# A decoder layer: the mask products leave TensorE, and the lambda steps go behind the last pair

## The chip, the cores and the metric

The kernel runs on one core of a Trainium2 chip. The metric is the device time of one execution in microseconds (us). A core has five engines with queues of their own: TensorE (PE, products, with PEld for its weight loads), VectorE (DVE), ScalarE (ACT), GpSimd (POOL) and SyncE (SP, which here only issues loads).

## The reference

One layer of a hybrid decoder for 512 tokens of width 1024. After a norm, a projection feeds eight stick-breaking heads and four differential heads, whose outputs go through `w_o`; then come a feed-forward part with a causal convolution, a gated embedding part and a last norm. The change concerns the stick-breaking heads, and the order of the lambdas of the differential heads:

```python
def block(args):                       # stick-breaking, one block of queries
    past = key_pos[None, :] < q_pos[:, None]
    z = einsum('bhqd,bhkd->bhqk', q_blk, k) * scale
    log_not = where(past, log_sigmoid(-z), 0.0)
    between = cumsum(log_not, axis=3, reverse=True) - log_not
    w = where(past, exp(log_sigmoid(z) + between), 0.0)
    return einsum('bhqk,bhkd->bhqd', w, v)
...
lam = exp(sum(lambda_q1 * lambda_k1)) - exp(sum(lambda_q2 * lambda_k2)) + lambda_init
w = probs[:, :, 0] - lam * probs[:, :, 1]     # differential heads
```

So the weight of key s for query t is sigmoid(z) times the product of sigmoid(-z) over the keys between s and t, and zero where s is not before t.

## The kernel before

Every 32-bit product is made as three products of split operands, high by high, high by low and low by high (`mm3`, L119 to L123). A weight block is loaded to `wraw`, cast to `whi` on ACT (L140), and the rest `wlo` is subtracted on DVE (L141). The text calls the three products of one 128x512 output and one block of 128 input rows a *unit*; the call `self.units(n)` takes the next n units from a flow of projection pieces: q and k of a pair of heads (`add_qk`, L377, its results scaled by DVE and split by ACT and DVE at L387 to L389), v of all pairs (`add_v`, L408, results split at L506 to L511), and so on, eight units for each q or k. PSUM has four banks of tag `mm` for units and two double banks of tag `z` for logits, transposes and head outputs.

A *pair* is two stick-breaking heads. `pair_steps` (L549) makes the logits of a pair in three groups of query blocks: block 3 (512 keys); blocks 2 and 0 (384 and 128 keys); block 1 (256 keys). `logits` (L482) ends a group with two products (L500), one for each head, of the identity with `maskR`, which add a large negative number at the unseen keys of the diagonal blocks. `sb_sticks` (L514) then works on a group: ACT makes sigmoid(-z) into `cum` (L524) and sigmoid(z) into `beta` (L525), DVE runs `cum` backwards as a running product that starts anew where `fresh` is one (a scan, L531, in pieces of 512), and multiplies `beta` by it (L532). Scans of groups 0 and 1 use the two `cum` buffers. `pair_out` (L561) transposes the result (L576), splits it (`split_t`, L542) and multiplies by v (L588), adds the parts of the two heads (L594, L595) and splits the output (L597, L598).

In `stages` (L713) PE follows the order in which the program is written: two units, the broadcast of the first norm to a row (`bcast_rstd1`, L154 and L158), the late evictions of q and k of pair 0, six units, and then a plan of steps of the four pairs with units between them (L820 to L827; an entry is pair, step, units). Other engines run in an order that a scheduler works out at build time; `issue_after` places work behind given instructions. `params` (L199 to L257) is called at one point of the plan (entry 8). It loads gains, convolution weights, lambdas and a one-hot table by loads that ACT issues (L229, L250), sums the lambda products on DVE (L233), takes exponentials on ACT (L238), and combines them (L241); it also makes the bias strips of the differential heads. These heads come after the pairs (`diff_steps`, L601).

Of the kernel before, what the change touches and what calls it, by code (L numbers as in the profile page):

```python
# [41 lines left out]
class Kern:  # L42
# [121 lines left out]
    def consts(self):  # L164
# [17 lines left out]
        zero = su.tile([P, P], F32, name="zero")  # L182
        nc.gpsimd.memset(zero, 0.0)
        msk = su.tile([P, P], F32, name="msk")

        nc.gpsimd.affine_select(msk, zero, pattern=[[-1, P]], compare_op=ALU.is_gt, fill=NEG, base=0, channel_multiplier=1)
        self.maskR = c.tile([P, P], F32R, name="maskR")
        nc.vector.tensor_copy(self.maskR, msk)
# [10 lines left out]
    def params(self, pst):  # L199
        nc, a, c = self.nc, self.a, self.cpool  # L200
# [12 lines left out]
        nc.scalar.dma_start(rows2[0 : 4 * FT, :], a["conv_w"][0, 1:3].rearrange("t (r p) -> (t r) p", p=P))  # L213
        self.par = c.tile([P, n1], F32, name="par1")
# [9 lines left out]


        rest = next(spare)
        lt = rest[:, : 4 * HD].rearrange("p (a d) -> p a d", a=4)
        for i, key in enumerate(("lambda_q1", "lambda_k1", "lambda_q2", "lambda_k2")):
            nc.scalar.dma_start(lt[:, i, :], a[key].partition_broadcast(P).rearrange("p o d -> p (o d)"))  # L229
        s = c.tile([P, 2], F32, name="lsum")  # L230
        junk = rest[:, 4 * HD : 5 * HD]
        for i in range(2):
            nc.vector.tensor_tensor_reduce(  # L233
                out=junk, in0=lt[:, 2 * i, :], in1=lt[:, 2 * i + 1, :], scale=1.0, scalar=0.0,
                op0=ALU.mult, op1=ALU.add, accum_out=s[:, i : i + 1],
            )
# [5 lines left out]


        tab = c.tile([NBUCK + 1, NMAP], F32, name="tab")
        nc.gpsimd.memset(tab, NEG)
        nc.scalar.dma_start(tab[0:NBUCK, :], a["rel_bias"])
        sk = self.dram.tile([NMAP, YW], F32, name="sk")
        for lo, n in ((0, T), (T, P)):
            oh, y = next(spare)[: NBUCK + 1, :n], next(spare)[:NMAP, :n]
            nc.scalar.dma_start(oh, a["onehot"][:, lo : lo + n])  # L250
# [6 lines left out]
        nc.scalar.dma_start(self.sk2, bass.AP(sk.tensor, sk.offset, [[YW, NMAP], [0, P], [1, YW]]))  # L257
# [78 lines left out]
    def behind_x(self, do):  # L336

        with self.tc.issue_after(self.last[0]), self.tc.issue_after(self.last[1]):
            do()
# [142 lines left out]
    def logits(self, q, k, blocks, mask=False):  # L482
# [4 lines left out]
        for at, (tb, col) in enumerate(blocks):  # L487
            n = (tb + 1) * P
            for i, (x, y) in enumerate(((0, 1), (1, 0), (0, 0))):
                for h in range(2):  # L490
# [3 lines left out]
                        start=i == 0 and at == 0, stop=i == 2 and at == len(blocks) - 1 and not mask, skip_group_check=True,  # L494
                    )
        if mask:

            d = [col // P + tb for tb, col in blocks]
            for h in range(2):
                nc.tensor.matmul(  # L500
                    z[:, h, :].rearrange("p (a b) -> p a b", b=P)[:, d[0] : d[-1] + 1, :], lhsT=self.identR,
                    rhs=self.maskR.unsqueeze(1).to_broadcast([P, len(d), P]), start=False, stop=True, skip_group_check=True,
                )
# [10 lines left out]
    def sb_sticks(self, z, g):  # L514
# [27 lines left out]
    def split_t(self, ps, n, c=""):  # L542
        nc = self.nc
        hi, lo = (x[:, :n] for x in self.parts("tw", c))
        nc.scalar.copy(hi, ps[:, :n])  # L545
        nc.vector.tensor_sub(lo, ps[:, :n], hi.bitcast(F32))  # L546
        return hi, lo

    def pair_steps(self, pair):  # L549
# [3 lines left out]
        zs = [self.logits(q, k, ((3, 0),), True), self.logits(q, k, ((2, 0), (0, 3 * P)), True)]  # L553
# [3 lines left out]
        self.sb_sticks(self.logits(q, k, ((1, 0),), True), 2)  # L557
# [155 lines left out]
    def stages(self):  # L713
# [56 lines left out]
        def begin(i):  # L770
            self.behind_x(lambda: self.prepare(i))
# [16 lines left out]
        self.behind_x(self.norm_x)  # L788
# [19 lines left out]
        self.fresh = self.work.tile([P, 6 * P], F32, name="fresh", bufs=1)  # L808
        nc.gpsimd.memset(self.fresh, 0.0)
        nc.gpsimd.memset(self.fresh[:, 3 * P : 3 * P + 1], 1.0)  # L810
        self.v[0] = self.vp.tile([P, NB, 2 * T], F32R, tag="v", name="v_sb")

        self.units(2)
# [19 lines left out]

# [219 lines left out]
```

## Time and profile before

| | before |
|---|---|
| median of 3 runs, us | 706.27 |
| lowest and highest, us | 704.77, 706.96 |
| profiled execution, us | 706.06 |
| its span, us | 704.3 |
| PE busy, us (share) | 685.5 (97%) |
| DVE busy, us (share) | 441.1 (63%) |
| ACT busy, us (share) | 313.8 (45%) |
| POOL busy, us (share) | 42.5 (6%) |

The span is counted from the first to the last event that the profiler recorded; the execution's own time is 1.8 us longer. In a row of a timeline the first number is the start in us, the second the duration; x6 means that six alike stand in the row together. The bracket gives the time for which the engine had been idle and who released it. A matmul's recorded duration overlaps the next one's start, so distances between starts tell the pace.

### The profile page before, as it was taken

The numbers are of one execution on the slowest core, as the hardware profiler recorded it, in microseconds if no ns is written. First come the engines' busy times: TensorE is split into PE (matmuls) and PEld (weight loads), VectorE is DVE, ScalarE is ACT, GpSimd is POOL, SyncE is SP. The second block draws the span as 40 slices with busy tenths as digits, with TensorE's granted clock in tenths as the row PEclk, the third lists the DMA queues.
The fourth block names the chain that finished last, engine by engine and source line by source line (L and its number), as shares of the span: only waits on it lengthen the run. The fifth ranks groups of instructions, "written<-read, shape, count | busy, mean of one in ns | idle before, by whom it ended". The sixth has DMA issues, their size and how long they took to land. (4 is left out here: it accounts for less than half of the span.)

```text
span 704.3 us, 8244 instructions
## 1 busy us (share of the span) xinstructions
PE 685.5 (97%) x3263; PEld 562.3 (80%) x3263; DVE 441.1 (63%) x663; ACT 313.8 (45%) x471; POOL 42.5 (6%) x52
## 2 busy tenths in 40 slices
PE   8879999999999999999999999999999999999995
PEld 8668877787888887888888888888888888888885
DVE  3775769668666858498777777677734232436445
ACT  4654435556553543365444444444423232326422
POOL 2200000000100024100000000000000020202001
PEclk9989999999999999999999999999999999999999
DMA  9522135232326111223322233321323133127002
GB/s 288 200 69 60 60 108 192 60 94 76 106 85 209 61 60 60 90 90 121 119 77 86 78 120 119 97 84 60 123 101 105 61 104 120 45 92 239 29 27 93
DMA packets 66809, 71.64 MB, mean 102 GB/s; under 512 B 2360, under 2 KB 55850, under 8 KB 66771
## 3 DMA queue, kind: packets, MB, share of 16 engines
q1 hardware_dynamic: 63376, 64.76, 28.8%
q10 hardware_dynamic: 2755, 4.27, 1.8%
q0 software_dynamic: 640, 2.10, 0.8%
q8 instruction: 25, 0.41, 0.3%
q14 instruction: 13, 0.11, 0.0%
HBM read 66.90 MB, written 6.84 MB: 105 GB/s over the span
## 5 line engine op out<-in xcount | busy, mean ns | idle before, releaser
L140 ACT CAST whi<-wraw 128x1024 fp32r<-128x1024 f32 (+1 forms) x102 | 105.5, 1034 | 151.0 <-PE mm L122 128.3
L141 DVE TENSOR_TENSOR wlo<-wraw,whi 128x1024 fp32r<-128x1024 f32 (+1 forms) x102 | 123.5, 1211 | 74.4 <-ACT whi L140 73.4
L121 PE MATMUL mm<-xgh,whi 128*128 128x512 f32 x128 | 53.9, 421 | 0.2 <-DVE v_sb L511 0.2
L122 PE MATMUL mm<-xgl,whi 128*128 128x512 f32 x128 | 51.6, 403 | 0.0
L123 PE MATMUL mm<-xgh,wlo 128*128 128x512 f32 x128 | 51.4, 401 | 0.0
L878 DVE TENSOR_TENSOR vpad<-mm,rb 128x512 f32<-128x512 f32 x44 | 30.1, 688 | 33.8 <-PE mm L123 33.7
L699 POOL TENSOR_TENSOR sqacc<-sqacc,sq 128x512 f32<-128x512 f32 x14 | 23.1, 1653 | 359.6 <-issue 254.9
L880 ACT ACTIVATE y<-vpad,par,par 128x512 f32<-128x512 f32 x44 | 35.5, 814 | 2.7 <-DVE vpad L878 2.5
L882 DVE SCALAR_TENSOR_TENSOR y<-vpad,par,y 128x512 f32<-128x512 f32 x44 | 33.1, 751 | 1.3
L881 DVE SCALAR_TENSOR_TENSOR y<-vpad,par,y 128x512 f32<-128x512 f32 x44 | 32.8, 746 | 0.0
L121 PEld LDWEIGHTS mm<-xgh,whi 128*128 128x128 f32 x128 | 25.2, 197 | 6.8 <-issue 1.1
L884 ACT ACTIVATE y<-y 128x512 f32<-128x512 f32 x22 | 13.9, 631 | 34.9 <-DVE y L882 34.9
L123 PEld LDWEIGHTS mm<-xgh,wlo 128*128 128x128 f32 x128 | 24.9, 194 | 5.6
L122 PEld LDWEIGHTS mm<-xgl,whi 128*128 128x128 f32 x128 | 25.1, 196 | 4.6 <-DVE xgl L331 0.3
L531 DVE TENSOR_TENSOR_SCAN cum<-cum,fresh 128x512 f32<-128x512 f32 x20 | 23.6, 1212 | 4.2 <-ACT cum L524 4.2
L492 PE MATMUL z<-k,q 64*128 64x512 f32 (+3 forms) x192 | 20.6, 340 | 5.2 <-ACT beta L525 3.7
L121 PE MATMUL mm<-whi,xgh 128*128 128x512 f32 x64 | 25.5, 398 | 0.0
L122 PE MATMUL mm<-wlo,xgh 128*128 128x512 f32 x64 | 25.0, 390 | 0.0
L123 PE MATMUL mm<-whi,xgl 128*128 128x512 f32 x64 | 25.0, 390 | 0.0
L492 PEld LDWEIGHTS z<-k,q 64*128 64x128 f32 x192 | 15.5, 189 | 10.9 <-ACT beta L525 4.2
L636 ACT ACTIVATE pr<-pr,nmx 128x512 f32<-128x512 f32 (+3 forms) x32 | 17.6, 552 | 12.2 <-DVE nmx L632 12.0
L546 DVE TENSOR_TENSOR twl<-z,twh 128x1024 fp32r<-128x1024 f32 (+2 forms) x20 | 18.4, 954 | 7.1 <-ACT twh L545 7.0
(538 smaller groups left out, 1759.4 us busy)
## 6 DMA issues: line engine op xcount, KB each, us to landing
wraw<-in_w_up SPq DMA_DIRECT2D x22, 1024.0 KB, 5.0
wraw<-in_w_in SPq DMA_DIRECT2D x16, 512.0 KB, 5.2
wraw<-in_w_down SPq DMA_DIRECT2D x8, 1024.0 KB, 5.0
wraw<-in_w_in SPq DMA_DIRECT2D x4, 1024.0 KB, 6.1
wraw<-in_w_o SPq DMA_DIRECT2D x4, 1024.0 KB
wraw<-in_w_ple_gate SPq DMA_DIRECT2D x4, 1024.0 KB, 8.2
wraw<-in_w_down SPq DMA_DIRECT2D x4, 768.0 KB, 4.3
sk<-sk ACTq DMA_DIRECT2D x1, 2560.0 KB
```

What stands on the lines that cost most here:

```text
L121: nc.tensor.matmul(ps, lhsT=l[0], rhs=r[0], start=start, stop=False, **kw)
L122: nc.tensor.matmul(ps, lhsT=l[0], rhs=r[1], start=False, stop=False, **kw)
L123: nc.tensor.matmul(ps, lhsT=l[1], rhs=r[0], start=False, stop=stop, **kw)
L140: nc.scalar.copy(hi, raw)
L141: nc.vector.tensor_sub(lo, raw, hi.bitcast(F32))
L492: nc.tensor.matmul(z[:, h, col : col + n], lhsT=q[o, x, tb * P : (tb + 1) * P], rhs=k[o, y, :n], start=i == 0 and at == 0, stop=i == 2 and ...
L531: nc.vector.tensor_tensor_scan(back, back, fresh, 1.0, op0=ALU.mult, op1=ALU.max)
L699: nc.gpsimd.tensor_add(sqacc, sqacc, sq)
L878: nc.vector.tensor_mul(u[:, 2 : T + 2], ps, rb2)
L880: nc.scalar.activation(y, u[:, 2 : T + 2], AF.Identity, scale=self.cw(2, ch), bias=self.g("cb", ch))
L881: nc.vector.scalar_tensor_tensor(y, u[:, 1 : T + 1], self.cw(1, ch), y, op0=ALU.mult, op1=ALU.add)
L882: nc.vector.scalar_tensor_tensor(y, u[:, 0:T], self.cw(0, ch), y, op0=ALU.mult, op1=ALU.add)
```

## The change

The products with `maskR` are gone. Instead, GpSimd builds two tables at the start: `keep`, a 128x128 block of ones where the key comes before the query and zeros elsewhere, and `whole`, which takes the place of `fresh` and has ones at the unseen keys of the diagonal blocks, so that the running product (a product followed by a maximum) is one there. The scans now cover a head's piece each, so the third group has two of 256 instead of one of 512. GpSimd multiplies the diagonal blocks of `beta` by `keep`, four-dimensional views of 128x2x128, 128x2x256 and 128x2x128 elements in the three groups, in place, between ACT's second sigmoid and DVE's product.

`params` becomes a generator whose loads are written at entry 4 of the plan and the rest at entry 8; the lambda steps have a function of their own, called after the split of v of the differential heads and placed behind the last split of a pair. PE gets five units instead of two ahead of the broadcast, and eight instead of eleven in the last entry of the plan.

```diff
-        zero = su.tile([P, P], F32, name="zero")
-        nc.gpsimd.memset(zero, 0.0)
-        msk = su.tile([P, P], F32, name="msk")
-
-        nc.gpsimd.affine_select(msk, zero, pattern=[[-1, P]], compare_op=ALU.is_gt, fill=NEG, base=0, channel_multiplier=1)
-        self.maskR = c.tile([P, P], F32R, name="maskR")
-        nc.vector.tensor_copy(self.maskR, msk)
+        self.keep = c.tile([P, P], F32, name="keep")
+        nc.gpsimd.affine_select(
+            self.keep, self.ones, pattern=[[-1, P]], compare_op=ALU.is_gt, fill=0.0, base=0, channel_multiplier=1
+        )
...
+        rest = next(spare)
+        lt = rest[:, : 4 * HD].rearrange("p (a d) -> p a d", a=4)
+        for i, key in enumerate(("lambda_q1", "lambda_k1", "lambda_q2", "lambda_k2")):
+            nc.scalar.dma_start(lt[:, i, :], a[key].partition_broadcast(P).rearrange("p o d -> p (o d)"))
...
+        yield
...
+    def lambdas(self):
+        nc, c = self.nc, self.cpool
+        s = c.tile([P, 2], F32, name="lsum")
+        for i in range(2):
+            nc.vector.tensor_tensor_reduce(
...
+        e = c.tile([P, 2], F32, name="lexp")
+        nc.scalar.activation(e, s, AF.Exp)
...
-        if mask:
-
-            d = [col // P + tb for tb, col in blocks]
-            for h in range(2):
-                nc.tensor.matmul(
-                    z[:, h, :].rearrange("p (a b) -> p a b", b=P)[:, d[0] : d[-1] + 1, :], lhsT=self.identR,
-                    rhs=self.maskR.unsqueeze(1).to_broadcast([P, len(d), P]), start=False, stop=True, skip_group_check=True,
-                )
...
-        for c0 in range(off, 2 * T, T):
-            back = c[:, c0 : c0 + T][:, ::-1]
-            r0 = (3 - g) * P
-            fresh = self.fresh[:, r0 : r0 + T] if g else self.fresh[:, 0:1].to_broadcast([P, T])
-            nc.vector.tensor_tensor_scan(back, back, fresh, 1.0, op0=ALU.mult, op1=ALU.max)
+        diag = two(beta).rearrange("p h (b k) -> p h b k", k=P)[:, :, (3, 2, 1)[g] :, :]
+        nc.gpsimd.tensor_mul(diag, diag, self.keep.unsqueeze(1).unsqueeze(1).to_broadcast(list(diag.shape)))
+
+
+        for c0 in range(off, 2 * T, w):
+            back = c[:, c0 : c0 + w][:, ::-1]
+            r0 = 0 if g == 1 else P
+            nc.vector.tensor_tensor_scan(back, back, self.whole[:, r0 : r0 + w], 1.0, op0=ALU.mult, op1=ALU.max)
...
-        nc.scalar.copy(hi, ps[:, :n])
-        nc.vector.tensor_sub(lo, ps[:, :n], hi.bitcast(F32))
+        a = nc.scalar.copy(hi, ps[:, :n])
+        b = nc.vector.tensor_sub(lo, ps[:, :n], hi.bitcast(F32))
+        self.last = (a.ins, b.ins)
...
+        self.whole = self.work.tile([P, 5 * P], F32, name="whole", bufs=1)
+        nc.gpsimd.memset(self.whole, 0.0)
+        for b in range(2):
+            w = self.whole[:, b * P : (b + 1) * P]
+            nc.gpsimd.affine_select(w, w, pattern=[[1, P]], compare_op=ALU.is_gt, fill=1.0, base=1 - P, channel_multiplier=1)
...
-        self.units(2)
+        self.units(5)
...
-            plan += [(p, 0, 3), (p, 1, 12), (p, 2, 4), (p, 3, 4), (p, 4, 4 if p == 2 else 11)]
+            plan += [(p, 0, 3), (p, 1, 12), (p, 2, 4), (p, 3, 4), (p, 4, 4 if p == 2 else 8)]
...
+            if i == 4:
+                params = self.params(self.psm)
+                next(params)
             if i == 8:
-                self.params(self.psm)
+                self.behind(lambda: next(params, None))
...
+        self.behind(self.lambdas)
```

The first place is ACT's row at pair 0, up to its first sigmoids. Before the change (L388 casts are the halves of q and k of a pair, L140 a weight cast, L229 and L250 issues of the loads of lambdas and one-hot table):

```order
L229 DMA mix4l_845<-in_lambda_k 128x64
L388 CAST k_386<-qkt_387 128x512
L229 DMA mix4l_845<-in_lambda_q 128x64
L229 DMA mix4l_845<-in_lambda_k 128x64
L250 DMA mix5h_846<-in_onehot 33x512
L250 DMA mix6h_848<-in_onehot 33x128
L238 ACTIVATE lexp<-lsum 128x2
L140 CAST whi_450<-wraw_247 128x1024
L388 CAST q_409<-qkt_410 128x512
L524 ACT_TABLE_LOAD
L524 ACTIVATE cum_341<-z_414 128x1024
L525 ACTIVATE beta_438<-z_414 128x1024
```

And the same place after the change:

```order
L393 CAST q_389<-qkt_390 128x512
L140 CAST whi_413<-wraw_241 128x1024
L216 DMA mix4l_659<-in_lambda_k 128x64
L393 CAST k_394<-qkt_395 128x512
L216 DMA mix4l_659<-in_lambda_q 128x64
L216 DMA mix4l_659<-in_lambda_k 128x64
L223 DMA mix5h_660<-in_onehot 33x512
L223 DMA mix5l_661<-in_onehot 33x128
L393 CAST q_408<-qkt_409 128x512
L521 ACT_TABLE_LOAD
L521 ACTIVATE cum_335<-z_427 128x1024
L522 ACTIVATE beta_447<-z_427 128x1024
```

The load issues stand where they stood, around k's cast; the exponential (L238) is gone from between them and the sigmoids, and the weight cast has come ahead of k's.

The second place is DVE at pair 0, from k's subtraction to the scans. Before (L233 and L241 are the lambda steps):

```order
L389 TENSOR_TENSOR k_386<-qkt_387,k_386 128x512
L233 ISA mix4l_845,lsum<-mix4l_845 128x64
L233 ISA lsum 128x1
L233 ISA mix4l_845,lsum<-mix4l_845 128x64
L233 ISA lsum 128x1
L241 SCALAR_TENSOR_TENSOR neglam<-lexp 128x1
L387 SCALAR_TENSOR_TENSOR qkt_410<-mm_359,rb_366 128x512
L141 TENSOR_TENSOR wlo_451<-wraw_247,whi_450 128x1024
L389 TENSOR_TENSOR q_409<-qkt_410,q_409 128x512
```

And after; the scans print as SCALAR_TENSOR_TENSOR, and qkt_491 is the eviction that frees a bank of units:

```order
L392 SCALAR_TENSOR_TENSOR qkt_409<-mm_358,rb_374 128x512
L141 TENSOR_TENSOR wlo_414<-wraw_241,whi_413 128x1024
L394 TENSOR_TENSOR k_394<-qkt_395,k_394 128x512
L394 TENSOR_TENSOR q_408<-qkt_409,q_408 128x512
L530 SCALAR_TENSOR_TENSOR cum_335<-cum_335,whole 128x512 x2
L531 TENSOR_TENSOR beta_447<-beta_447,cum_335 128x1024
L530 SCALAR_TENSOR_TENSOR cum_336<-cum_336,whole 128x512 x2
L531 TENSOR_TENSOR beta_454<-beta_454,cum_336 128x1024
L530 SCALAR_TENSOR_TENSOR cum_335<-cum_335,whole 128x256 x2
L392 SCALAR_TENSOR_TENSOR qkt_491<-mm_417,rb_374 128x512
```

The lambda steps have gone, and the eviction of q and the weight split now stand ahead of k's subtraction.

The third place is DVE at pair 1, between the scans and the first v eviction. Before:

```order
L531 SCALAR_TENSOR_TENSOR cum_341<-cum_341,fresh 128x512 x2
L532 TENSOR_TENSOR beta_633<-beta_633,cum_341 128x1024
L531 SCALAR_TENSOR_TENSOR cum_342<-cum_342,fresh 128x512 x2
L532 TENSOR_TENSOR beta_639<-beta_639,cum_342 128x1024
L531 SCALAR_TENSOR_TENSOR cum_341<-cum_341,fresh 128x512
L532 TENSOR_TENSOR beta_663<-beta_663,cum_341 128x512
L141 TENSOR_TENSOR wlo_678<-wraw_502,whi_677 128x1024
L511 SCALAR_TENSOR_TENSOR v_sb<-mm_505,rstd_268,v_sb 128x8x64
```

And after:

```order
L530 SCALAR_TENSOR_TENSOR cum_335<-cum_335,whole 128x512 x2
L531 TENSOR_TENSOR beta_635<-beta_635,cum_335 128x1024
L530 SCALAR_TENSOR_TENSOR cum_336<-cum_336,whole 128x512 x2
L141 TENSOR_TENSOR wlo_694<-wraw_499,whi_693 128x1024
L530 SCALAR_TENSOR_TENSOR cum_335<-cum_335,whole 128x256
L531 TENSOR_TENSOR beta_642<-beta_642,cum_336 128x1024
L530 SCALAR_TENSOR_TENSOR cum_335<-cum_335,whole 128x256
L508 SCALAR_TENSOR_TENSOR v_sb<-mm_502,rstd_262,v_sb 128x8x64
```

The weight split has come ahead of group 1's multiply, whose place is now between the two short scans, and group 2's multiply has gone behind the v eviction.

## Rows read from the trace of the kernel before

**Rows 1.** The page's part 1: busy time, share and instructions of each engine.

```profile
PE 685.5 (97%) x3263; PEld 562.3 (80%) x3263; DVE 441.1 (63%) x663; ACT 313.8 (45%) x471; POOL 42.5 (6%) x52
```

**Rows 2.** What PE waits for: us in total, times, longest.

```profile
PE z L492 <- DVE av L595: 0.6, 1, 0.6
PE z L576 <- DVE beta L532: 0.4, 1, 0.4
```

**Rows 3.** PE's timeline, from the norm's broadcast to past pair 0's logits.

```profile
29.45 0.33 PE L158 MATMUL z<-identR,bch 128*128 128x128 f32 x1 [2.12 <-DVE bch L154]
...
34.84 0.96 PE L492 MATMUL z<-k,q 64*128 64x512 f32 x6
...
43.45 1.01 PE L492 MATMUL z<-k,q 64*128 64x256 f32 x6 [3.75 <-ACT beta L525]
...
49.14 0.39 PE L122 MATMUL mm<-xgl,whi 128*128 128x512 f32 x1
```

**Rows 4.** Windows: us, busy (x) of PE, PEld, DVE, ACT, POOL, PEclk, DMA share, GB/s.

```profile
39.70:43.40 3.70, 0.00 (x1) 0.00 (x0) 2.68 (x3) 3.67 (x5) 0.00 (x0) 0.83 0.32 93
43.40:45.00 1.60, 1.55 (x9) 1.33 (x10) 1.50 (x3) 1.60 (x2) 0.00 (x0) 0.50 1.18 322
...
26.00:29.00 3.00, 1.34 (x6) 0.76 (x5) 2.56 (x6) 2.06 (x5) 1.58 (x2) 1.00 0.62 171
```

**Rows 5.** ACT's timeline at pair 0 (ACTq: its queue issues a load).

```profile
33.38 0.41 ACTq L229 DMA_DIRECT2D mix4l<-in_lambda_q  x1
...
34.74 0.36 ACTq L250 DMA_DIRECT2D mix6h<-in_onehot  x1
38.49 0.20 ACT L238 ACTIVATE lexp<-lsum 128x2 f32<-128x2 f32 x1 [4.51 <-DVE lsum L233]
...
39.54 0.61 ACT L388 CAST q<-qkt 128x512 fp32r<-128x512 f32 x1
40.16 1.28 ACT L524 ACT_TABLE_LOAD   x1
41.46 1.02 ACT L524 ACTIVATE cum<-z 128x1024 f32<-128x1024 f32 x1
```

**Rows 6.** PE's timeline in pair 1, and the first differential head's logits.

```profile
64.91 0.97 PE L492 MATMUL z<-k,q 64*128 64x512 f32 x6
...
67.53 0.39 PE L121 MATMUL mm<-whi,xgh 128*128 128x512 f32 x1
...
69.68 0.62 PE L492 MATMUL z<-k,q 64*128 64x256 f32 x6
...
70.51 0.45 PE L121 MATMUL mm<-whi,xgh 128*128 128x512 f32 x1
...
78.44 0.50 PE L121 MATMUL mm<-xgh,whi 128*128 128x512 f32 x1 [0.22 <-DVE v_sb L511]
...
164.53 1.77 PE L492 MATMUL z<-k,q 64*128 64x512 f32 x18 [0.76 <-DVE k L389]
166.23 0.50 PE L121 MATMUL mm<-xgh,whi 128*128 128x512 f32 x1
```

**Rows 7.** DVE's timeline at pair 1.

```profile
67.40 2.34 DVE L531 TENSOR_TENSOR_SCAN cum<-cum,fresh 128x512 f32<-128x512 f32 x2 [1.46 <-ACT cum L524]
...
74.57 1.22 DVE L531 TENSOR_TENSOR_SCAN cum<-cum,fresh 128x512 f32<-128x512 f32 x1
...
76.50 1.22 DVE L141 TENSOR_TENSOR wlo<-wraw,whi 128x1024 fp32r<-128x1024 f32 x1
77.64 2.72 DVE L511 SCALAR_TENSOR_TENSOR v_sb<-mm,rstd,v_sb 128x512 fp32r<-128x512 f32 x4
```

**Rows 8.** GpSimd's timeline, an addition of 512 elements a row.

```profile
643.72 1.30 POOL L699 TENSOR_TENSOR sqacc<-sqacc,sq 128x512 f32<-128x512 f32 x1 [5.09 <-ACT sq L698]
```

**Rows 9.** DVE's timeline: one step (two inputs in SBUF) at two places.

```profile
608.39 0.74 DVE L693 SCALAR_TENSOR_TENSOR h25l<-hT,par,h25h 128x512 fp32r<-128x512 f32 x1
...
643.79 1.78 DVE L693 SCALAR_TENSOR_TENSOR h27l<-hT,par,h27h 128x512 fp32r<-128x512 f32 x1
```

More of the change, by code (lines that the diff above doesn't have):

```diff
@@ L213, in params @@
         nc.scalar.dma_start(rows2[0 : 4 * FT, :], a["conv_w"][0, 1:3].rearrange("t (r p) -> (t r) p", p=P))
+        rest = next(spare)
+        lt = rest[:, : 4 * HD].rearrange("p (a d) -> p a d", a=4)
+        for i, key in enumerate(("lambda_q1", "lambda_k1", "lambda_q2", "lambda_k2")):
+            nc.scalar.dma_start(lt[:, i, :], a[key].partition_broadcast(P).rearrange("p o d -> p (o d)"))
+        tab = c.tile([NBUCK + 1, NMAP], F32, name="tab")
+        nc.gpsimd.memset(tab, NEG)
+        nc.scalar.dma_start(tab[0:NBUCK, :], a["rel_bias"])
+        hot = {}
+        for lo, n in ((0, T), (T, P)):
+            hot[lo] = next(spare)[: NBUCK + 1, :n]
+            nc.scalar.dma_start(hot[lo], a["onehot"][:, lo : lo + n])
+        yield
         self.par = c.tile([P, n1], F32, name="par1")
@@ L223, in params @@
         nc.vector.tensor_scalar(self.gsub, self.g("sub", 0), 1.0 - LAMBDA_INIT, None, op0=ALU.mult)
[L226 to L235, printed above, removed]
-            )
-        e = c.tile([P, 2], F32, name="lexp")
-        nc.scalar.activation(e, s, AF.Exp)
-        self.neglam = c.tile([P, 1], F32, name="neglam")
-        nc.vector.scalar_tensor_tensor(self.neglam, e[:, 1:2], -LAMBDA_INIT, e[:, 0:1], op0=ALU.add, op1=ALU.subtract)
-        tab = c.tile([NBUCK + 1, NMAP], F32, name="tab")
-        nc.gpsimd.memset(tab, NEG)
-        nc.scalar.dma_start(tab[0:NBUCK, :], a["rel_bias"])
+        self.lt, self.junk = lt, rest[:, 4 * HD : 5 * HD]
         sk = self.dram.tile([NMAP, YW], F32, name="sk")
         for lo, n in ((0, T), (T, P)):
-            oh, y = next(spare)[: NBUCK + 1, :n], next(spare)[:NMAP, :n]
-            nc.scalar.dma_start(oh, a["onehot"][:, lo : lo + n])
+            oh, y = hot[lo], next(spare)[:NMAP, :n]
             ps = pst()
@@ L334, in prep_x, with behind @@
             yield banks
-    def behind_x(self, do):
+    def behind(self, do):
         with self.tc.issue_after(self.last[0]), self.tc.issue_after(self.last[1]):
@@ L479, in half_out, with logits @@
             self.nc.vector.tensor_add(self.hT[nt], ps, self.hT[nt])
-    def logits(self, q, k, blocks, mask=False):
+    def logits(self, q, k, blocks):
         nc = self.nc
@@ L493, in logits @@
                         z[:, h, col : col + n], lhsT=q[o, x, tb * P : (tb + 1) * P], rhs=k[o, y, :n],
-                        start=i == 0 and at == 0, stop=i == 2 and at == len(blocks) - 1 and not mask, skip_group_check=True,
+                        start=i == 0 and at == 0, stop=i == 2 and at == len(blocks) - 1, skip_group_check=True,
                     )
-        if mask:
-            d = [col // P + tb for tb, col in blocks]
-            for h in range(2):
-                nc.tensor.matmul(
-                    z[:, h, :].rearrange("p (a b) -> p a b", b=P)[:, d[0] : d[-1] + 1, :], lhsT=self.identR,
-                    rhs=self.maskR.unsqueeze(1).to_broadcast([P, len(d), P]), start=False, stop=True, skip_group_check=True,
-                )
         return z
@@ L552, in pair_steps @@
         self.at = {}
-        zs = [self.logits(q, k, ((3, 0),), True), self.logits(q, k, ((2, 0), (0, 3 * P)), True)]
+        zs = [self.logits(q, k, ((3, 0),)), self.logits(q, k, ((2, 0), (0, 3 * P)))]
         for g in range(2):
@@ L556, in pair_steps @@
         yield
-        self.sb_sticks(self.logits(q, k, ((1, 0),), True), 2)
+        self.sb_sticks(self.logits(q, k, ((1, 0),)), 2)
         yield
@@ L770, in begin @@
         def begin(i):
-            self.behind_x(lambda: self.prepare(i))
+            self.behind(lambda: self.prepare(i))
             if i < 2:
@@ L787, in stages @@
         begin(2)
-        self.behind_x(self.norm_x)
+        self.behind(self.norm_x)
         for k in range(2, KT):
```

8 lines of the change are left out of this document (5 added, 3 removed).

## The prediction

> **What bounds the kernel now.** I read the page's busy times first: PE is busy 685.5 us of a span of 704.3, every other engine under two thirds [rows 1]. The end is therefore set by the number and speed of products, plus the few places where PE stands. The list of what PE waits for gives those places; the ones in the stick-breaking stretch (about 27 to 170 us) are all that this change can touch. Two short ones at its end are in [rows 2]; the two long ones are seen best in PE's timeline: 2.12 us before the broadcast of the first norm (27.3 to 29.45, released by `bch`) and 3.75 us before the last logits of pair 0 (39.7 to 43.45, released by the sigmoid of L525) [rows 3]. The windows tell of the clock. [...] PE was standing before the clock fell.
>
> The price of that fall: from 43.45 to 49.14, 5.69 us, PE runs the last logits and mask products of pair 0 and ten products of 512 columns [rows 3]. At full clock the same logits and masks take 0.83 in pair 1 (69.68 to 70.51), and nine products ahead of them 2.15 (67.53 to 69.68), 0.23 each and a hand-over, so ten take 2.3 [rows 6]. The loss is 5.69 − 2.3 − 0.83 = 2.6 us.
>
> The 3.75 wait has its cause on ACT: it stands 4.51 us for the lambda sums, then runs `lexp`, a weight cast, q's cast and a table load of 1.28 before the sigmoid at 41.46 [rows 5]. These lambda steps are what the change moves.
>
> **The change part by part.** The sum is made against the profiled execution's 706.06 (span 704.3 and 1.8 around it); the median is 706.27, so the two are 0.2 apart.
>
> *Mask products.* 24 go, 6 a pair. In pair 1 the first two groups' logits with masks run from 64.91 to 67.53, 2.62. The logits of a diff head, same products without masks, take 164.53 to 166.23, 1.70 [rows 6]. So 0.92 for 512 of the 512 + 256 mask columns that I count as two thirds, and near 0.3 for the third group by its share of columns; I take 0.2 off, since the product behind them loses its overlap: 1.0 a pair, **−4.0** for four. All of it is on PE, hence on the path.
>
> *Three units earlier.* A unit is three products. PE gets three more ahead of the broadcast and three fewer in the last plan, so the count is the same, and 3 x 0.68 = 2.05 us of products now fill the 2.12 wait: **−1.9** (0.1 stays, 0.1 for the hand-over).
>
> *Lambda steps moved behind pair 3.* ACT now goes from k's cast (beside the issue at 33.38 in the trace, about 33.6 with a weight cast ahead of it) through four load issues (three of them take from 33.38 to 34.74, so 0.45 each, which ends at 35.4), q's cast 0.61 and the table 1.28 [rows 5]: the sigmoid starts at 37.3 instead of 41.46. Beta is there at 39.2, before PE needs its bank (39.85). The wait goes with the clock's loss: −3.75 − 2.6 = **−6.35**. The exponential itself lies behind pair 3, where DVE and ACT have products of several units beside them: nothing.
>
> *What is late next.* On DVE a weight split (1.22 in [rows 7]) now stands ahead of k's subtraction. PE waited 0.12 for k before 34.84; now some 1.2: **+1.1**, logits at 35.95.
>
> The next PSUM bank that is late is that of the last v column block: it comes free with the q/k eviction that DVE runs behind the scans of all three groups. DVE: first scan at 37.3 + 1.02 = 38.3; two groups of scans and multiplies take 7.17 (67.40 to 74.57); two half scans 2 x 0.6; the eviction 0.68 [rows 7]; together 47.4. PE: 35.95 + 1.8 (logits of two groups) + 2.1 (three units) + 0.65 (third group) + 5.5 (eight units) = 46.0. A new wait of 1.4: **+1.4**.
>
> The same after pair 1. Before, PE reached the bank at 78.44, 13.5 behind its logits (64.91), and waited 0.22 for the v eviction [rows 6]. Now it comes 1.2 sooner for the masks and 2.05 sooner for the three units, at 10.1 to 10.2 behind them, while DVE ends that eviction at 12.25: 2.1 (first scan, its z 0.4 earlier than at 67.40) + 7.17 + 1.2 + 1.2 (split and two half scans; the multiply goes behind) + 0.68, less 0.1. A wait of 2.2, **+2.0**.
>
> Smaller: a logits bank of pair 1, +0.3; pair 2, +0.9 for two evictions between the additions of the heads, less 0.40 and 0.65 that end [rows 2], so +0.15; the first diff head's logits, where k is 0.76 late [rows 6] and PE now comes 2.05 sooner with two DVE steps of 0.6 gone, +0.85. Together **+1.3**.
>
> Sum so far: −4.0 − 1.9 − 6.35 + 1.1 + 1.4 + 2.0 + 1.3 = −6.45, so **699.6**.
>
> *GpSimd's product on beta.* Twelve operations, 256, 512 and 256 elements a row in each pair. The nearest row on GpSimd is 1.30 for 512 elements [rows 8]; so 0.65, 1.30 and 0.65. GpSimd is idle in this stretch, and each operation can start when the sigmoid of beta has ended, in the first scan; DVE's multiply waits for it and behind that multiply stand the scans and the evictions just listed. The question is whether scans and GpSimd run side by side. No row shows a scan beside GpSimd. The nearest: a DVE step with two inputs in SBUF takes 0.74 alone and 1.78 when it starts 0.07 behind GpSimd's operation [rows 8, 9]; it lost 1.04. A scan has two inputs in SBUF as well. Lower bound 0, as both may overlap and a gain has no mechanism; upper bound the whole GpSimd operations, 2.6 a pair; I take 1.04 for 512 and half of it for 256, 2.08 a pair, by the nearest row. Where DVE is what PE waits for, it counts in full: 1.4 becomes 3.5, 2.2 becomes 4.3, and pair 3's transposes wait 1.45 that was hidden (the other 0.6 is covered). Pair 2 has cover enough. **+5.6**, so 705.2.
>
> [...]
>
> *The clock.* A wait of 2.12 kept it and one of 3.75 lost it [rows 3, 4]. The wait of 4.3 is longer than the one that lost it, so I count one fall, at the price that this trace shows, 2.6. That of 3.5 lies between and I count none. 705.2 + 2.6 = **707.8**.
>
> The rest is at nothing: the scans are as many elements as before, 24 pieces for 20; the tables `keep` and `whole` are made on GpSimd before anything needs them; the loads of the parameters stand at the same place in ACT's queue.
>
> **The rivals.** *Two falls.* The wait after pair 0, 3.5, loses the clock too. It decides at a length between 2.12 and 3.75, and 3.5 is near the upper end, so it may well: 707.8 + 2.6 = 710.4, slower than before. If the GpSimd operation blocks a scan for its whole length, that is 1.5 more, 711.9. For it: only 0.25 us lies between this wait and the one that is known to have lost the clock. Against it: hand-summed chains of ten steps are no better than 0.5.
>
> [...]
>
> [...]
>
> *The change does not do what it says* can be put aside in the main: the order of the instructions shows the lambda steps behind pair 3 and PE three units ahead; only the parameter loads, written as moved, stay.
>
> **How the numbers follow.** One fall, 707.8: 0.34, with its own range 706.3 to 709.3 (the 0.5 of each chain and the 0.2 to 0.3 of the profiled execution). Two falls, 710.4: 0.20. Lock without fall, 705.2: 0.14. No lock or half, 699.6 to 702.4: 0.32. A measurement of this kernel tells some 0.3% from no change, so faster means below 704.15 and slower above 708.4. Faster: 0.30 of the last case and 0.03 of the third, 0.33. Slower: 0.20 and 0.11 of the forecast's upper end, 0.31. Same: 0.36. The range goes from 698.5 (699.6 less one new wait that does not come) to 711.5 (two falls with most of the longer lock); what is left out is some 0.07 at either end.
>
> **What would show it.** [...] ACT's sigmoid near 37.3 and no wait on beta before 40 would show the lambda step right. PE's waits should be near 0.1 for `bch`, 1.2 for k, 3.5 on a q/k eviction near 46 and 4.3 on a v eviction after pair 1, with the clock at 0.50 behind the second alone. No waits over 1.5 at either place would make the forecast wrong to the low side; a clock of 0.50 twice, to the high side.

## The result and the profile after

| | before | after |
|---|---|---|
| median, us | 706.15 | 711.07 |
| lowest and highest, us | 704.77, 706.96 | 710.94, 713.06 |
| profiled execution, us | 706.06 | 713.06 |
| its span, us | 704.3 | 711.3 |

The changed kernel is slower: the ratio is 1.0076, with an interval of 1.0056 to 1.0096. The forecast was 707.8, no change that can be told; the time lies near the rival of two falls of the clock, 710.4, and inside the range of 698.5 to 711.5. The profiled execution is 2 us above the kernel's other runs; the run of the changed kernel again returns to that.

The page's part 1 of the changed kernel (answers to [rows 1]):

```profile
PE 682.8 (96%) x3239; PEld 559.9 (79%) x3239; DVE 448.6 (63%) x666; ACT 313.3 (44%) x471; POOL 57.3 (8%) x64
```

PE is busy 2.7 us less, although 4 us of mask products are gone (part of what is left runs at a granted clock of 0.50, as the windows below show), and DVE is busy 7.5 us more, although it works on as many elements as before. What PE waits for, the longest (us in total, times, longest; answers to [rows 2]):

```profile
PE mm L121 <- DVE qkt L392: 5.2, 2, 2.9
PE z L497 <- DVE k L394: 3.9, 2, 2.1
PE mm L121 <- DVE v_sb L508: 3.9, 1, 3.9
...
PE z L576 <- DVE beta L531: 1.4, 1, 1.4
```

All are on DVE. PE's timeline has them in order of time (answers to [rows 3] and [rows 6]; the bracket is the wait):

```profile
28.99 0.33 PE L158 MATMUL z<-identR,bch 128*128 128x128 f32 x1 [0.73 <-DVE bch L154]
...
36.52 2.50 PE L497 MATMUL z<-k,q 64*128 64x512 f32 x18 [2.14 <-DVE k L394]
38.95 0.79 PE L121 MATMUL mm<-xgh,whi 128*128 128x512 f32 x1
...
51.19 0.80 PE L121 MATMUL mm<-whi,xgh 128*128 128x512 f32 x1 [2.88 <-DVE qkt L392]
...
65.36 1.78 PE L497 MATMUL z<-k,q 64*128 64x512 f32 x18
67.06 0.50 PE L121 MATMUL mm<-whi,xgh 128*128 128x512 f32 x1
...
79.47 0.80 PE L121 MATMUL mm<-xgh,whi 128*128 128x512 f32 x1 [3.89 <-DVE v_sb L508]
...
124.02 0.50 PE L121 MATMUL mm<-whi,xgh 128*128 128x512 f32 x1 [2.30 <-DVE qkt L392]
...
153.71 1.94 PE L576 MATMUL z<-ident,beta 128*128 128x128 f32 x16 [1.43 <-DVE beta L531]
...
171.40 1.78 PE L497 MATMUL z<-k,q 64*128 64x512 f32 x18 [1.79 <-DVE k L394]
```

The first differential head's logits start at 171.40 where they started at 164.53 before [rows 6]: 6.9 of the 7.0 us between the two profiled executions have arisen by then. The 3.75 us wait on beta [rows 3] is gone, as forecast, and five new ones of 1.4 to 3.9 stand in its place. The windows of the three stretches after a wait (us, busy (x) of the five engines, PEclk, DMA share, GB/s; answers to [rows 4]) show a granted clock below 1.00 in each. The 0.66 of the first is made up of 1.00 up to 37.00, 0.78 to 37.50 and 0.50 from there to 38.95; behind the other two, from 54.34 and from 85.14, it is 0.99 and 1.00 again:

```profile
36.52:38.95 2.43, 2.43 (x18) 2.27 (x19) 0.69 (x1) 1.59 (x2) 0.00 (x0) 0.66 0.61 161
...
51.19:54.34 3.15, 3.15 (x8) 2.50 (x8) 2.28 (x3) 0.78 (x2) 0.00 (x0) 0.50 0.04 8
79.47:85.14 5.67, 5.67 (x13) 4.51 (x14) 3.65 (x5) 0.00 (x0) 0.00 (x0) 0.51 0.27 104
```

With 0.23 for a product of 512 columns and 1.70 for the logits of two groups, the three falls cost 1.6 (logits and the four products up to 40.77, 4.25 in place of 2.62), 1.5 (seven products, 3.15 in place of 1.6) and 2.7 (thirteen, 5.67 in place of 3.0): 5.8, where the one of before cost 2.6.

DVE's timeline at pair 0 tells why PE waits. The second fence has the second of its first two scans by itself, the third GpSimd's products:

```profile
40.33 2.84 DVE L530 TENSOR_TENSOR_SCAN cum<-cum,whole 128x512 f32<-128x512 f32 x2 [1.64 <-ACT cum L521]
43.27 2.23 DVE L531 TENSOR_TENSOR beta<-beta,cum 128x1024 f32<-128x1024 f32 x1
45.42 2.33 DVE L530 TENSOR_TENSOR_SCAN cum<-cum,whole 128x512 f32<-128x512 f32 x2
47.85 1.51 DVE L531 TENSOR_TENSOR beta<-beta,cum 128x1024 f32<-128x1024 f32 x1
```

```profile
41.47 1.70 DVE L530 TENSOR_TENSOR_SCAN cum<-cum,whole 128x512 f32<-128x512 f32 x1
```

```profile
41.29 0.80 POOL L524 TENSOR_TENSOR beta<-beta,keep 128x256 f32<-128x256 f32 x1 [13.07 <-ACT beta L522]
43.12 1.30 POOL L524 TENSOR_TENSOR beta<-beta,keep 128x512 f32<-128x512 f32 x1 [1.04 <-ACT beta L522]
46.76 1.53 POOL L524 TENSOR_TENSOR beta<-beta,keep 128x256 f32<-128x256 f32 x1 [2.34 <-ACT beta L522]
```

Two scans took 2.34 before [rows 7]; here the pair beside the first product takes 2.84. The multiply that starts at 43.27, 0.15 behind a product of 1.30, takes 2.23. No bracket stands at the multiplies: DVE does not stand and wait for GpSimd, its instructions get longer. It goes the other way too: the third product has as many elements as the first and takes 1.53 in place of 0.80, beside DVE's scans.

In these rows the instruction that starts second is the one that gets longer. The first scan, begun ahead of the first product, takes its 1.22; the second, begun at 41.47 behind it, takes 1.70. The kernel before has the same pattern in a row that was taken for one of an undisturbed step: beside the 0.74 at 608.39 [rows 9], GpSimd started 0.11 later and took 1.79, where the one that started first took 1.30 [rows 8]:

```profile
608.50 1.79 POOL L699 TENSOR_TENSOR sqacc<-sqacc,sq 128x512 f32<-128x512 f32 x1 [2.41 <-ACT sq L698]
```

### The profile page after: what moved, and what is told of

It is laid out like the page before. It is cut to its first block, busy times and chain, and to the rows that moved or that the text cites. A ratio compares the mean times of both kernels' runs of the same rounds, so it can differ in the third digit from the quotient of the medians.

```text
span 711.3 us, 8222 instructions
## 1 busy us (share of the span) xinstructions
PE 682.8 (96%) x3239; PEld 559.9 (79%) x3239; DVE 448.6 (63%) x666; ACT 313.3 (44%) x471; POOL 57.3 (8%) x64
## 5 line engine op out<-in xcount | busy, mean ns | idle before, releaser
L141 DVE TENSOR_TENSOR wlo<-wraw,whi 128x1024 fp32r<-128x1024 f32 (+1 forms) x102 | 124.7, 1222 | 73.0 <-ACT whi L140 71.9
L140 ACT CAST whi<-wraw 128x1024 fp32r<-128x1024 f32 (+1 forms) x102 | 105.4, 1034 | 143.0 <-PE mm L122 115.3
L530 DVE TENSOR_TENSOR_SCAN cum<-cum,whole 128x512 f32<-128x512 f32 (+1 forms) x24 | 26.3, 1132 | 5.4 <-ACT cum L521 5.4
```

Of the source, the lines that this page charges most:

```text
L140: nc.scalar.copy(hi, raw)
L141: nc.vector.tensor_sub(lo, raw, hi.bitcast(F32))
L530: nc.vector.tensor_tensor_scan(back, back, self.whole[:, r0 : r0 + w], 1.0, op0=ALU.mult, op1=ALU.max)
```

## The experiments

Theory 1: GpSimd's product, by slowing DVE in the stretch in which PE waits for DVE ("the lock" in the forecast's cases and below), costs the most, directly and through the clock. Rivals: the loads' issue that stands before k's cast on ACT; PE's lead of three units; DVE waiting for GpSimd, not being slowed by it. Ratios are against the kernel before, run beside each.

**The product left out.** Edit of the changed kernel:

```diff
-        nc.gpsimd.tensor_mul(diag, diag, self.keep.unsqueeze(1).unsqueeze(1).to_broadcast(list(diag.shape)))
```

> The changed kernel without GpSimd's product on the diagonal blocks of beta (left out: the unseen keys of the diagonal blocks keep their weight). Theory 1 (GpSimd's product, through the scans and multiplies of DVE that it slows and holds, costs the most): the scan pairs that took 2.84 go back to 2.34 and the multiplies that took 2.23 and 1.51 to 1.23; PE's waits of 2.88, 3.89 and 1.43 shrink to about 0.8, 1.8 and 0, with the clock kept at the first two places, so 711.1 falls to 702 to 703.5. Rival (the wait for k, 2.14, and the fall of the clock behind it, or PE's being three units ahead, cost the most): the waits keep most of their length and the time stays above 707.5.

Measured: 703.35, ratio 0.9963 (0.9948 to 0.9979), 7.7 below the changed kernel. The waits of 2.88, 3.89, 2.30 and 1.43 are 1.81, 1.86, 0.45 and none, and scans of 512 and large multiplies are back at 1.21 and 1.22 on the mean. The product is what costs; the first wait shrank less than expected. The clock was not kept, as had been expected, but fell at other places: behind a wait for the broadcast of 1.51 (0.50 from 32 to 34 us) and behind the wait of 1.86 (0.50 from 76 to 78).

**A write in its place.** GpSimd waits for the same sigmoid and DVE for GpSimd, as before, but GpSimd reads nothing:

```diff
-        nc.gpsimd.tensor_mul(diag, diag, self.keep.unsqueeze(1).unsqueeze(1).to_broadcast(list(diag.shape)))
+        nc.gpsimd.memset(diag, 0.0)
```

> The changed kernel with GpSimd's product replaced by a write of zeros to the same diagonal blocks at the same place, so that the order of waits is kept and only GpSimd's reading of SBUF goes (the diagonal blocks' weights are left out). If the loss comes from both engines reading SBUF: no DVE instruction of pair 0 is longer than beside an idle GpSimd (scan pair 2.34, multiplies 1.23), time 702 to 704.5. If it comes from GpSimd's being there at all, or from DVE's multiply waiting for it: scans and multiplies stay long or stand, 708 to 711.

Measured: 700.99, ratio 0.9926 (0.9900 to 0.9952), 10.1 below the changed kernel. DVE's groups over the four pairs (30 to 160 us; busy us, mean ns), first of the changed kernel, then of this one:

```profile
L530 DVE TENSOR_TENSOR_SCAN cum<-cum,whole 128x512 f32<-128x512 f32 x16 | 20.7, 1332 | 5.4 <-ACT cum L521 5.4
L141 DVE TENSOR_TENSOR wlo<-wraw,whi 128x1024 fp32r<-128x1024 f32 x15 | 19.2, 1281 | 5.7 <-ACT whi L140 5.7
L531 DVE TENSOR_TENSOR beta<-beta,cum 128x1024 f32<-128x1024 f32 x8 | 14.1, 1759 | 0.4
...
L530 DVE TENSOR_TENSOR_SCAN cum<-cum,whole 128x256 f32<-128x256 f32 x8 | 5.7, 733 | 0.0
```

```profile
L141 DVE TENSOR_TENSOR wlo<-wraw,whi 128x1024 fp32r<-128x1024 f32 x16 | 19.5, 1219 | 4.5 <-ACT whi L140 4.5
L530 DVE TENSOR_TENSOR_SCAN cum<-cum,whole 128x512 f32<-128x512 f32 x16 | 18.7, 1210 | 5.4 <-ACT cum L521 5.4
L531 DVE TENSOR_TENSOR beta<-beta,cum 128x1024 f32<-128x1024 f32 x8 | 9.8, 1221 | 0.5
...
L530 DVE TENSOR_TENSOR_SCAN cum<-cum,whole 128x256 f32<-128x256 f32 x8 | 5.1, 674 | 0.0
```

Beside a GpSimd that only writes, DVE runs as fast as in the run without the product (1210, 1221 and 674 ns on the mean for scans of 512, large multiplies and scans of 256, where that run has 1210, 1222 and 675). The product adds 2.0 and 0.6 to the scans and 4.3 to the large multiplies; a weight split of 1.28 on the mean in place of 1.22 makes 0.9 more. That is 7.8 over four pairs, 1.95 a pair. PE's waits fall from 2.88, 3.89, 2.30 and 1.43 to 1.16, 1.85, 0.44 and none, 7.05 in all, so nearly the whole of DVE's loss was PE's. The rest of the 10.1 is put down to the clock (this kernel's profile has one fall, far on, from 158 to 164 us, at 0.68, 0.50 and 0.97 in steps of 2 us, the changed kernel's has three) and to the wait for k (1.32 here); it was not measured by itself. DVE standing and waiting for GpSimd is ruled out by the last column: DVE is idle for 0.4 us in all ahead of the eight large multiplies with the product, and for 0.5 with the write.

That it is the reading, and not the length or the moment, is not isolated by this run. The write takes 0.53 where the product takes 1.30, and in all four pairs it begins behind the multiply and not ahead of it:

```profile
40.34 1.23 DVE L531 TENSOR_TENSOR beta<-beta,cum 128x1024 f32<-128x1024 f32 x1
```

```profile
40.67 0.53 POOL L524 MEMSET beta<- 128x512 f32 x1 [1.51 <-ACT beta L522]
```

**One input in place of two.**

```diff
-        nc.gpsimd.tensor_mul(diag, diag, self.keep.unsqueeze(1).unsqueeze(1).to_broadcast(list(diag.shape)))
+        nc.gpsimd.affine_select(
+            diag, diag, pattern=[[0, 2], [0, diag.shape[2]], [-1, P]], compare_op=ALU.is_gt, fill=0.0, base=0, channel_multiplier=1
+        )
```

> The changed kernel with GpSimd's product replaced by its select against an affine pattern, on the same blocks in place: one input read from SBUF (beta) instead of two (beta and the table of ones). If any reading by GpSimd stops DVE's second input: DVE's multiplies and scans stay long in proportion to GpSimd's time, 706 to 711. If it is the second input of GpSimd that does it: DVE as beside an idle GpSimd, 700 to 702.5, as with the write alone.

Measured: 705.06 (701.25 to 706.36), ratio 0.9972 (0.9954 to 0.9991): neither value; its profile is of an execution of 702.78, shorter than the median. The scans of 512 are still long, the multiplies are not:

```profile
L532 DVE TENSOR_TENSOR_SCAN cum<-cum,whole 128x512 f32<-128x512 f32 x16 | 21.4, 1378 | 5.4 <-ACT cum L521 5.4
L533 DVE TENSOR_TENSOR beta<-beta,cum 128x1024 f32<-128x1024 f32 x8 | 9.7, 1218 | 0.5
```

So beside a select, which reads one input, the scans took longer too, 1378 ns on the mean in place of 1210: 2.7 us in all instead of 7.8. The rows point to the moments for the multiplies that escaped: in pairs 0 and 1 the large select begins 0.17 behind the multiply, where the product began 0.15 ahead of it. In pair 0 the scan pair that follows, begun at 40.99 while the select still ran, took 2.95. No run has a select that begins ahead of a multiply, so that it would slow one is not shown.

```profile
39.84 1.23 DVE L533 TENSOR_TENSOR beta<-beta,cum 128x1024 f32<-128x1024 f32 x1
```

```profile
40.01 1.56 POOL L524 TENSOR_SCALAR_AFFINE_SELECT beta<-beta 128x512 f32<-128x512 f32 x1 [1.34 <-ACT beta L522]
```

**The lambda steps alone.** The kernel before, with the sums, the exponential and the difference in a function that is called behind the last split of pair 3:

```diff
-        e = c.tile([P, 2], F32, name="lexp")
-        nc.scalar.activation(e, s, AF.Exp)
...
+        self.behind_x(self.lambdas)
```

> The kernel before with one thing changed: the lambda sums, exponential and difference stand behind the last split of pair 3; masks, units and loads as before. If the 3.75 wait and the fall of the clock behind it are due to the lambda steps, as the prediction has it: wait below 0.3, clock at full through pair 0, 706.1 falls by about 6.3 to 699.8. If other work on ACT (the loads' issues, the table load) takes their place, a wait of 1.5 or more stays at that place and the time is above 702.

Measured: 701.71, ratio 0.9935 (0.9920 to 0.9950). The 3.75 wait is 0.32, the granted clock is 1.00 through all four pairs (in each step of 2 us from 20 to 166), and the gain is 4.4 (5.5 between the two profiled executions, 706.06 and 700.60, the second the fastest of its four). The mechanism holds, the size of 6.35 does not quite: 0.32 of the wait stays, and a new one of 0.38 stands behind the scans.

**The mask products back.** The changed kernel with the mask products, `fresh` and its scans as before, and no product:

```diff
-        nc.gpsimd.tensor_mul(diag, diag, self.keep.unsqueeze(1).unsqueeze(1).to_broadcast(list(diag.shape)))
...
-        for c0 in range(off, 2 * T, w):
+        for c0 in range(off, 2 * T, T):
...
+        if mask:
```

> The changed kernel with the mask products on TensorE again, the scans as in the kernel before and no product on GpSimd; the moved lambda steps and units stay. Theory 1: PE gets back 4.0 us of products, DVE loses 1.8 to 2.6 us a pair, so the waits of 2.88 and 3.89 fall to below 1.0 each with the clock kept, while the wait of 2.14 for k stays with its fall: 702 to 704. Rival (units and loads are at fault, not the product): waits over 2 remain at both places and the time is above 708, since the 4.0 us are added.

Measured: 701.34, ratio 0.9932 (0.9917 to 0.9947), a little below what was expected. No wait on pair 0's scans is left, the one after pair 1 is 1.18, and k is waited for 1.36 instead of 2.14. Behind that short wait the clock fell all the same:

```profile
35.80 0.96 PE L500 MATMUL z<-k,q 64*128 64x512 f32 x6 [1.36 <-DVE k L397]
```

```profile
38.00:40.00 2.00, 2.00 (x13) 1.69 (x10) 1.77 (x2) 1.78 (x3) 0.00 (x0) 0.50 1.07 297
```

**The units back.** The changed kernel with the old numbers:

```diff
-        self.units(5)
+        self.units(2)
...
-            plan += [(p, 0, 3), (p, 1, 12), (p, 2, 4), (p, 3, 4), (p, 4, 4 if p == 2 else 8)]
+            plan += [(p, 0, 3), (p, 1, 12), (p, 2, 4), (p, 3, 4), (p, 4, 4 if p == 2 else 11)]
```

> The changed kernel with two units ahead of the broadcast and eleven in the last entry, as before. If PE's three units of lead only move waits from the broadcast to the scans (DVE sets the pace of this stretch): the broadcast's wait comes back at about 2, the waits of 2.88 and 3.89 shrink by about 2 in all or each, those at pair 2 and 3 stay, fewer falls of the clock: 708.5 to 711. If the lead is worth its 1.9 as the prediction counted: 712.5 to 713.5. If the lead itself causes the loss: below 707.

Measured: 708.14 (705.70 to 709.96), ratio 1.0026 (1.0008 to 1.0044), just below the range for a lead that only moves waits. The broadcast's wait is 3.31, with the clock at 0.50 behind it (32 to 34 us), those behind the scans 2.20 and 2.48 with the clock at 1.00 behind them; pair 2 waits 2.37 at its transposes, and pair 3's wait is gone. This profile is of the fastest of ten executions (705.70), and the mean granted clock of the others is lower (0.988 to 0.993 against 0.995), so most of them lost more clock than it shows. With the run with the masks back and the one with the lambda steps alone it makes a table, all with the lambda steps moved:

| median, us | two and eleven units | five and eight |
|---|---|---|
| mask products on PE | 701.71 | 701.34 |
| product on GpSimd | 708.14 | 711.07 |

The swap of masks for the product costs 6.4 with the old units and 9.7 with the new. The three units of lead are worth 0.4 where DVE keeps up, and cost 2.9 where it doesn't: PE arrives sooner at the same late DVE. That the clock goes to 0.50 there with the lead and stays at 1.00 without is what the two profiles show; for the other executions it is not shown.

**The loads late.** The first part of the parameters' loads goes behind the last split of pair 0:

```diff
-                next(params)
+                self.behind(lambda: next(params))
```

> The changed kernel with the first part of the parameters' loads placed behind the last split of pair 0, so that ACT issues none of them ahead of k's cast and the weight load of that stretch has the queues for itself. If the wait of 2.14 for k comes from the load issue that stands before k's cast on ACT and waits for a weight load that lands late: k's cast starts at about 33.3, the wait falls to 0.5 to 1.2 and the clock stays at full there, a gain of 2.5 to 3.5, but the waits behind scans stay or grow: 707.5 to 709. If the load issue only marks a time that is set by the split ahead of k: 2 us of wait remain and the time is 710.5 to 711.5.

Measured: 709.82, ratio 1.0053 (1.0038 to 1.0068), 1.25 below the changed kernel and between the two ranges expected. The wait for k is 1.37, near the 1.2 of the prediction, and no fall follows it (1.00 from 34 to 56 us); the waits of 2.65, 3.85, 2.33 and 1.44 stay. So the loads make 0.8 of that wait, and they are a small part of the loss. They do so only in some executions: with the loads in their place k is waited for 1.36 with the masks back, 1.32 with the write and 1.36 with the select. With the masks back as well, nothing is left of it:

> The changed kernel with mask products on TensorE as in the run with the masks back, and the loads late. The run with the masks back has 701.3 with waits of 1.36 for k and 1.18 for v, and one fall. If late loads take the fall away and half of the wait for k: 698.5 to 700.5. If the loads were no part of it: 701 to 702; if they collide later (pair 1's sigmoids stand behind their issue on ACT): above 702.

Measured: 701.43, ratio 0.9933 (0.9909 to 0.9958), the same as with the masks back alone; k is waited for 1.34.

**The changed kernel again.**

> The changed kernel once more, unchanged: its profiled execution was 2 us above its other runs. If those 2 us are one of its three falls of the clock, a profile at 711 shows the same waits within 0.3 and one fall fewer or shorter ones. If the waits themselves differ between executions, it shows other waits.

Measured: 710.90 (709.27 to 714.73), ratio 1.0065 (1.0038 to 1.0093). The profiled execution, at 714.73, has the waits behind scans at 3.07, 3.88, 2.31 and 1.45, the same within 0.2, and again three falls (0.50 from 40 to 42, 54 to 56 and 80 to 86 us); but k is waited for 2.66 and the broadcast 1.51, which makes most of the 1.67 between the two profiles. Again the profiled execution is the slowest of its run, so there is no profile near 711, and the question as it was put stays without an answer. The mean granted clocks of all nine executions help: 0.987 in the three slowest (713.06, 713.45, 714.73), 0.989 to 0.992 in the six others. By an estimate from these, 0.002 to 0.005 of 711 us, the others lost 1.4 to 3.6 us less to the clock; the first fall cost 1.6. So they had a fall fewer or shorter ones; which one is not shown. In both profiles the weight load issued at that time lands late. Ahead of k's cast ACT has the issue of a lambda load, which starts at the moment at which the weight load lands (34.63 here; so it was in the other runs with that order):

```profile
26.84 0.42 ACTq L216 DMA_DIRECT2D mix4l<-in_lambda_q  x1
...
34.63 0.35 ACTq L216 DMA_DIRECT2D mix4l<-in_lambda_k  x1
35.03 0.62 ACT L393 CAST k<-qkt 128x512 fp32r<-128x512 f32 x1 [1.78 <-DVE wlo L141]
```

The weight load is issued at 26.84 too, and lands 7.8 us later (8.3 in the second execution, issued at 27.77 beside a lambda load at 27.76, and 7.6 in the run without the product, both issued at 27.79). Where the lambda load was issued some 0.45 behind the weight load (the runs with the masks back, the write and the select) it landed in 5.4, 5.9 and 5.7 us, and in 5.5 before. That the small load issued in the same moment delays it is what these rows suggest; no run changed that alone.

**A version without mask products and without the product.** The weight of a key, sigmoid(z) times the product of sigmoid(-z) over the later keys, is the difference of two neighbouring running products, and it is zero of itself where the product is one. Only the last column of each diagonal block, whose right neighbour belongs to another piece, is set to zero by GpSimd:

```diff
-        nc.scalar.activation(two(beta), z[:, :, :w], AF.Sigmoid)
...
-        nc.gpsimd.tensor_mul(diag, diag, self.keep.unsqueeze(1).unsqueeze(1).to_broadcast(list(diag.shape)))
...
-        nc.vector.tensor_mul(beta, beta, c[:, off + 1 : 2 * T + 1])
+        nc.vector.tensor_sub(beta, c[:, off + 1 : 2 * T + 1], c[:, off : 2 * T])
+        last = two(beta).rearrange("p h (b k) -> p h b k", k=P)[:, :, (3, 2, 1)[g] :, P - 1 : P]
+        nc.gpsimd.memset(last, 0.0)
```

> Loads late as in the run of that name; the weights are taken as differences of neighbouring running products (sigmoid(z) times the product to the right of s is that product less the one that takes in s), so that beta's sigmoids on ACT and GpSimd's product go, DVE subtracts where it multiplied, and GpSimd only writes zeros to the last column of each diagonal block, behind DVE. Theory 1: this is the run with late loads (709.8) less the lock, 7.7 as measured by the run without the product: 701 to 703. If ACT's beta sigmoids were part of what DVE waited for, it is better than that, below 700. If the waits behind the scans come from DVE's own work and not from the lock: above 705.

Measured: 698.94, ratio 0.9892 (0.9864 to 0.9921): 7.2 below the kernel before, 12.1 below the changed one, and the fastest of all. Its waits:

```profile
PE z L497 <- DVE k L394: 3.2, 2, 1.8
...
PE mm L121 <- DVE v_sb L508: 1.8, 1, 1.8
...
PE z L497 <- DVE av L594: 0.8, 1, 0.8
PE mm L121 <- DVE qkt L392: 0.7, 1, 0.7
```

Against the run with late loads (709.82) it gains 10.9, more than the 7.7 that was counted. That fits the 10.1 of the write, and 0.8 is left that the missing sigmoids may or may not have given, although the time is below the 700 that had been put down to them. Against late loads with masks (701.43), the version without mask products is 2.5 faster, not 4.0: part of what PE saves it waits for (0.74 and 1.84 at the banks, where it was 0.16 and 1.39), and behind the 1.84 the clock fell in its profile (0.56 and 0.59 in the steps of 2 us from 72 to 76). The two also differ in how the weights are made, so 2.5 is not the products' worth alone.

## Where the prediction held and where it failed

Two terms of the sum failed in the main: pair 2's share of what DVE loses beside GpSimd's product, which was put at nothing and measured 1.9, and the clock, which was one fall at 2.6 where the profiles have two behind scans, at 1.5 and 2.7, and one more behind the late k. Term by term:

- **Mask products, −4.0.** In pair 1 the logits of two groups take 1.70 (65.36 to 67.06) where they took 2.62 [rows 6]: the 0.92 of the prediction. Right as PE's own time; by the last comparison 2.5 of it came through. The count of columns beside it was off (two groups have 768 of a pair's 1024 mask columns, three quarters), but the 0.3 for the third group is what the right count gives.
- **Three units, −1.9.** The broadcast's wait is 0.73 and 1.51 in the two profiles, 1.51 without the product, and none in the six other runs with the new units. But the lead itself is worth 0.4 (with masks) or −2.9 (with the product). The step that failed is to count it as a gain by itself: PE was given work ahead of a stretch in which DVE sets the pace.
- **Lambda steps, −6.35.** 4.4 by the medians, 5.5 by the profiles. Wait and fall went as told.
- **k, 1.2.** 1.37 with late loads; 2.14 and 2.66 in the two profiles. The step that failed: ACT's load issues were counted at 0.45 each from 33.6, as in [rows 5]; the first of them came at 34.63, when a weight load had landed. Where that load landed early, the 1.2 was right (1.32 to 1.36).
- **"Smaller", +1.3.** In it pair 2 counts +0.15, but 0.9 less 0.40 and 0.65 is −0.15; the sum was 0.3 too high by this slip.
- **The waits behind the scans.** Without DVE's loss beside the product the prediction had 1.4 and 2.2, and the write gave 1.16 and 1.85; with it 3.5 and 4.3, measured 2.88 and 3.89; for pair 3's transposes 1.45, measured 1.43. The chains held within 0.6.
- **GpSimd's product, 2.08 a pair.** 1.95, and a scan of 512 took 1.22 or, begun behind the product, 1.70. The runs show longer durations; what holds DVE up in them is not shown. The sum was right, the places were not: multiplies bear more than half of it (4.3 of 7.8), where scans had been named. That the sums agree is in part luck. The row of 0.74 was not "alone", as the text had it; DVE had started first there.
- **"Pair 2 has cover enough."** It had not: 2.30, and 0.44 with the write. This step failed: it put pair 2's share at nothing without a reason from a row, and it is 1.9; 7.05 of PE's waiting hang on the product, where 5.6 were counted.
- **One fall.** The profiles have three, at 1.6, 1.5 and 2.7, so 5.8 where 2.6 was counted. The step that failed is to place the fall by the length of a wait, between 2.12 and 3.75. Waits of 1.36 (masks back), 1.51 and 1.86 (no product), 1.84 (difference) and 2.14 were followed by a fall (the lowest step of 2 us at 0.50 to 0.56), and those of 2.30 (pair 2), 2.20 and 2.48 (units back) were not (1.00); of two waits of 2.65 the one with the select was (0.55), the one with late loads was not (1.00). So the length alone does not tell, and what does stays open here. Pair 2's 1.9 and the second fall's 1.5 are together 3.4, the size of the forecast's error (711.07 less 707.8, 3.3); that they meet it so closely is luck in part, since the other deviations (−0.6 and −0.4 at the scans, −0.3 for the slip, +0.9 where k was late) are of both signs and only in part cancel. The third of the falls counted here, the one of 1.6, stands behind the late k. Both profiled executions are the slowest of their runs and the others have the higher mean clock, so I take it that the others had k in time; no profile of such a run of this kernel shows it.

## What to carry to other kernels

Work taken from PE for an idle GpSimd was not free here, where VectorE is what PE waits for: VectorE's scans and multiplies that began behind a GpSimd product took longer (a scan of 512 1.70 in place of 1.22, a multiply 2.23 in place of 1.23), and so did scans beside a select (1.38 on the mean). So price it as VectorE time (here 7.8 us over four pairs), ask which of the two starts first, and look for it in the durations, since no wait showed it here (0.4 us of idle time in all ahead of the eight large multiplies). Before moving PE's work ahead, find which engine sets the pace behind it; here a lead that ended at a later wait gained nothing. A mask can be implied by the algebra: the difference of running products needed neither the mask products nor GpSimd's multiplication, only a write of zeros to one column of each diagonal block.

## What the runs showed of the hardware that was not expected

The conversion of the identity at the start, a copy with one input, took 0.98 in the changed kernel, beside GpSimd's select for `keep` (0.29) and its write of `whole` (0.63), and 0.23 in the kernel before, where GpSimd's next select began 0.04 behind it:

```profile
1.58 0.98 DVE L181 CAST identR<-ident 128x128 fp32r<-128x128 f32 x1 [1.58 <-POOL ident masks.py:199]
```

```profile
1.83 0.63 POOL L809 MEMSET whole<- 128x640 f32 x1
```

The kernel before shows a write alone beside such a copy, that of the mask, which has the same size and took 0.77:

```profile
2.04 0.77 DVE L188 CAST maskR<-msk 128x128 fp32r<-128x128 f32 x1 [0.18 <-POOL msk L186]
```

```profile
1.96 0.73 POOL L809 MEMSET fresh<- 128x768 f32 x1
```

So beside a write of GpSimd that began 0.08 ahead of it a copy of DVE took 0.77 in place of 0.23, although beside the short writes above scans and multiplies took no longer (1210 and 1221 ns). PE's first products came at 2.63 instead of 1.91. And the clock: it was at 0.50 behind a wait of 2.88 in the changed kernel, and behind one of 1.36 with the masks back, while with late loads it stayed at 1.00 through a wait of 2.65:

```profile
48.00:52.00 4.00, 3.17 (x14) 2.60 (x15) 3.49 (x6) 1.67 (x2) 0.00 (x0) 1.00 0.03 6
75.00:82.00 7.00, 6.38 (x15) 4.98 (x16) 4.28 (x6) 0.00 (x0) 0.00 (x0) 0.52 0.30 116
```

The second row, the same run with its wait of 3.85, has the fall.
